# A hybrid attention block on one core: the key and value compression as whole fp32 products, two positions to a pass, with the positional encoding as extra columns

## The chip, the cores and the metric

The kernel runs on one core of a Trainium2 chip. The metric is the device time of one execution in microseconds (us); before the change it was run three times, and the median counts. The profile is of one further execution. Engine names: PE is TensorE's matmul queue and PEld its weight loads, DVE is VectorE, ACT is ScalarE, POOL is GpSimd, SP is SyncE, whose queue issues nearly all transfers. L12 is line 12 of the kernel file. "Granted clock" is the share of full speed that TensorE's clock was allowed.

## What is computed

One layer on a sequence of 1024 positions of width 1024: a mixer of two kinds of sparse attention, cross-attention to a memory of 256 rows, and an MLP of width 4096, each behind an RMS norm and added to the residual. The mixer projects the normed input with one wide matrix and splits the result. Only a small piece of it is touched by the change, the compressed keys and values of the second kind of attention:

```python
n_cmp = (L - CMP_BLOCK) // CMP_STRIDE + 1          # 63 blocks of 32 positions, stride 16
tok = jnp.arange(n_cmp)[:, None] * CMP_STRIDE + jnp.arange(CMP_BLOCK)[None, :]
k_blocks = k_br[:, :, 0][:, tok] + nsa_cmp_pe[0][:, None, :]
v_blocks = v_br[:, :, 0][:, tok] + nsa_cmp_pe[1][:, None, :]
k_c = jnp.einsum('bnlgd,lde->bnge', k_blocks, w_nsa_cmp[0])
v_c = jnp.einsum('bnlgd,lde->bnge', v_blocks, w_nsa_cmp[1])
k_c = _rope(_rms_norm(k_c, nsa_kn_g[0]), cmp_end)
```

So for keys and for values (kv = 0, 1), each of two heads g and each block n, 32 positions of 64 features, with an encoding of the position in the block added, are multiplied by 32 matrices of 64 x 64 and summed. The queries then attend to the 63 results, to selected blocks and to a window; the other kind of attention selects 256 positions by an index score. All inputs and outputs are fp32.

## The kernel before

**Number formats.** Most products are made in a reduced fp32 format of the PE (F32R in the code). An operand x is split into hi, its rounded copy, and lo = x - hi, and a product of two split operands is three matmuls: hi x hi, hi x lo, lo x hi. `split_w` (L240) splits weights: ACT makes hi, and POOL or DVE lo, by a rotating plan. Where both operands are left in plain F32 the product is one `matmul` in the code; these are called whole, and the projections of the second part and the output projections are done so (`load_whole`, L261). L218 is the helper through which every matmul passes, so in the profile nearly all of them carry this line and are told apart by their tiles.

**Stages.** The sequence is cut into two parts of four tiles of 128 positions (`PARTS`, L27). `project(pool, part, ...)` norms and transposes the part's input, and runs the wide projection in chunks of 256 columns (`gemm`, L300), handing each result bank to `consume`. Part 0 runs alone, in pool p1. Then attention starts on its tiles, and `together` (L110) interleaves it with a stream of other work, `fill`: the projection of part 1 (pool p2), the memory's projections, output projections, cross-attention and the MLP of the first four tiles. Every step of a generator announces a number (its rough cost), and `together` keeps attention and the other stream in proportion by these numbers and by `PACES` (1.35 for the first tiles). Attention's tile 3 is not begun before part 1 has been projected. The order in each engine's queue is settled when the kernel is built, by the tile framework's scheduler, which also inserts the waits.

**The compression.** Chunk 4 of the projection (columns 968 to 1223) holds the raw keys and values of the compressed branch. `consume` doubles each head's 64 features to 128 columns (L431), transposes (L434), and writes `KT[kv]`: features on the partitions, positions along the free dimension, hi on partitions 0 to 63 (ACT, L438, which writes all 128) and lo on 64 to 127 (DVE, L439). A matmul over 128 partitions so adds the products of hi and of lo in one pass, if the weights stand twice, above and below.

`compress` (L494) then goes over kv. It loads the 32 matrices as two tiles of 16, each transfer made twice for the upper and the lower half (L505), splits them in pieces of four positions (L511; ACT, POOL, DVE), and for each of the 16 offsets l in a stride of 16 multiplies by hi and by lo. The 128 weight columns are the matrices of position l and position l + 16, j = 0 and 1. The moving operand is `KT[kv][:, :, l::16]`, every sixteenth position, 64 columns in all for two heads and 32 strides (L515). Where part is 0, the same weights also multiply the encoding `pe`, two columns (L517), for the bias `cb` that both parts use. The two halves of the result, shifted by a block, are added to `cT` (L525 to L530), transposed, normed and rotated (keys) or split (values).

In part 0, `alternate` sends one projection tile of chunks 5 and 6 (8 tiles) and one step of `compress` (10 steps) by turns; in part 1 the two follow each other. In the profile the compression's bank is psC in part 0 and psD in part 1, `KT` is called c (tag c8, shared with other tiles), its weights come from tiles x (tag x4), and the encoding's bank is psM.

`pe_stack` (L1061) transposes the encoding at the start and splits it like `KT`.

Of the kernel before, what the change touches and what calls it, by code (L numbers as in the profile page):

```python
# [9 lines left out]
F32 = mybir.dt.float32  # L10
F32R = mybir.dt.float32r
# [11 lines left out]
P = 128  # L23
# [143 lines left out]
def build(nc, tc, I, C, out):  # L167
# [17 lines left out]
    def ring(pool, tag, shape, dt=F32):  # L185
        n = RINGS[pool.name if isinstance(pool.name, str) else "dn"][tag]
        return pool.tile(shape, dt, tag=tag, name=tag, bufs=n)
# [29 lines left out]
    def mm(o, a, b, start, stop):  # L217
        te.matmul(o, a, b, start=start, stop=stop)  # L218
# [149 lines left out]
    def project(pool, part, pe, st):  # L368
# [36 lines left out]
        def consume(ci, t, pt):  # L405
            T = t0 + t
            if ci in (0, 1):
                w = 256 if ci == 0 else 128
                gn = cqg if ci == 0 else ckvg
                ss = small(pool, "css", 1)  # L410
                raw = ring(pool, "relu", [P, 2, 256])
                s.activation(raw[:, 1, :w], pt[:, :w], AF.Square, accum_out=ss)
                s.activation(raw[:, 0, :w], pt[:, :w], AF.Copy)
                r = rsqrt_of(pool, ss, w, 1, "c")
                v.scalar_tensor_tensor(raw[:, 1, :w], raw[:, 0, :w], r[:, 0:1], gn, op0=ALU.mult, op1=ALU.mult)
                dst = [c[:, t, :, :] for c in cq] if ci == 0 else [c[:, t:t + 1, :] for c in ckv]
                to_T(pool, raw[:, 1, :], dst, w // P)
            if ci == 1:
                mu = small(pool, "mu", 1)
                v.tensor_reduce(mu, pt[:, 128:192], axis=AX.X, op=ALU.add)  # L420
                v.tensor_scalar(mu, mu, -1.0 / 64, None, op0=ALU.mult)
                v.tensor_scalar(kraw[t][:, IDX, :], pt[:, 128:192], mu[:, 0:1], None, op0=ALU.add)
                v.tensor_scalar(st["wi"][:, T, :], pt[:, 192:200], IDX_SCALE, None, op0=ALU.mult)
                s.activation(st["gi"][:, T, :], pt[:, 200:224], AF.Exp, scale=-1.0)
                v.tensor_scalar(st["gi"][:, T, :], st["gi"][:, T, :], 1.0, None, op0=ALU.add)
                v.reciprocal(st["gi"][:, T, :], st["gi"][:, T, :])
            if ci in (2, 3):
                stage_q(1, ci - 2, t, pt)
            if ci == 4:
                kd = ring(pool, "relu", [P, 4, 2, 64])  # L430
                s.activation(kd, pt.rearrange("p (a d) -> p a d", d=64)[:, :, None, :].to_broadcast([P, 4, 2, 64]), AF.Copy)  # L431
                p2 = pst("M", [P, 4, P])
                for a in range(4):
                    te.transpose(p2[:, a, :], kd[:, a, :, :].rearrange("p b d -> p (b d)"), ident)  # L434
                for kv in range(2):
                    dst = KT[kv][:, :, t * P:(t + 1) * P]
                    src = p2[:, kv * 2:kv * 2 + 2, :]
                    s.activation(dst, src, AF.Copy)  # L438
                    v.tensor_tensor(dst[64:128], src[64:128], dst[64:128], op=ALU.subtract)  # L439
            if ci in (5, 6):  # L440
                b = ci - 5
                V = st["V"][b]
                s.activation(kraw[t][:, 2 * b:2 * b + 2, :], pt[:, :128].rearrange("p (a d) -> p a d", d=64), AF.Copy)
                split_ps(pt[:, 128:256].rearrange("p (a d) -> p a d", d=64), V[:, T, :, 0, :], V[:, T, :, 1, :])
# [33 lines left out]
                    v.tensor_tensor(dst[64:128], p2[64:128], dst[64:128], op=ALU.subtract)  # L478
                yield 1.0

        KT += [ring(pool, "c8", [P, 2, nt * P], F32R) for _ in range(2)]
        yield from w_in([[(968, 256)]], 4)
        yield from w_in([[(0, 256)], [(256, 200), (1736, 24)]], 0)
        pair_ = (w_in([[(1224, 256)], [(1480, 256)]], 5), compress(pool, part, KT, pe, st, ctab))
# [9 lines left out]
    def compress(pool, part, KT, pe, st, ctab):  # L494
        t0, nt = PARTS[part]
        m0, nm = t0 * 8, nt * 8
        wc = W["w_nsa_cmp"].rearrange("k l d e -> k d l e")
        for kv in range(2):
            cp = pst(TAGS[pool.name][2], [P, 2, nm])
            pp = pst("M", [P, 2]) if part == 0 else None  # L500
            raws = []
            for j in range(2):
                raw = ring(pool, "x4", [P, 16, 64])
                for dup in range(2):
                    nc.sync.dma_start(raw[dup * 64:dup * 64 + 64], wc[kv][:, j * 16:j * 16 + 16, :])  # L505
                raws.append(raw)
            for rr in range(4):
                hi, lo = ring(pool, "whi", [P, 4, P], F32R), ring(pool, "wlo", [P, 4, P], F32R)
                for j in range(2):
                    js = slice(j * 64, j * 64 + 64)  # L510
                    split_w(raws[j][:, rr * 4:rr * 4 + 4, :], hi[:, :, js], lo[:, :, js])  # L511
                for r in range(4):
                    l = rr * 4 + r
                    for a, w in enumerate((hi, lo)):
                        mm(cp, w[:, r, :], KT[kv][:, :, l::16], l == 0 and a == 0, l == 15 and a == 1)  # L515
                    for a, w in enumerate((hi, lo) if part == 0 else ()):
                        mm(pp, w[:, r, :], pe[:, kv, l::16], l == 0 and a == 0, l == 15 and a == 1)  # L517
                yield 1.0
            cb = st["cb"][kv]
            if part == 0:  # L520
                b1 = small(pool, "cb1", 1, p=64)
                s.activation(b1, pp[64:128, 1:2], AF.Copy)
                v.tensor_tensor(cb, pp[0:64, 0:1], b1, op=ALU.add)
            cT = st["cT"][kv]
            s.activation(cT[:, :, m0:m0 + nm], cp[0:64], AF.Identity, bias=cb[:, 0:1])  # L525
            c1 = ring(pool, "relu", [P, 2, nm])[0:64]
            s.activation(c1, cp[64:128], AF.Copy)
            skip = 1 if part == 0 else 0
            dst = cT[:, :, m0 + skip - 1:m0 + nm - 1]
            v.tensor_tensor(dst, dst, c1[:, :, skip:], op=ALU.add)  # L530
            p2 = pst("M", [P, P])
            if kv == 0:
                te.transpose(p2[:, 0:64], cT.rearrange("p a n -> p (a n)"), ident[0:64, 0:64])
                ta = ring(pool, "relu", [P, 6, 64])
                ss = small(pool, "kcss", 1)
                s.activation(ta[:, 0, :], p2[:, 0:64], AF.Copy)
                s.activation(ta[:, 1, :], p2[:, 0:64], AF.Square, accum_out=ss)
                r = rsqrt_of(pool, ss, 64, 1, "kc")
                v.tensor_tensor(ta[:, 1, :], ta[:, 0, :], ctab[:, 0, :], op=ALU.mult)
                v.tensor_tensor(halves(ta[:, 2, :]), swap(ta[:, 0, :]), halves(ctab[:, 1, :]), op=ALU.mult)  # L540
                v.tensor_tensor(ta[:, 1, :], ta[:, 1, :], ta[:, 2, :], op=ALU.add)
                kcd = ta[:, 4:6, :]
                v.tensor_scalar(kcd, ta[:, 1:2, :].to_broadcast([P, 2, 64]), r[:, 0:1], None, op0=ALU.mult)
                p3 = pst("M", [P, 2, 64])
                te.transpose(p3.rearrange("p a n -> p (a n)"), kcd.rearrange("p a n -> p (a n)"), ident)
                Kc = st["Kc"][part] = at.tile([P, 2, 64], F32R, tag="Kc", name="Kc", bufs=len(PARTS))
                s.activation(Kc, p3, AF.Copy)
                v.tensor_tensor(Kc[64:128], p3[64:128], Kc[64:128], op=ALU.subtract)
            else:
                Vc = st["Vc"][part] = at.tile([64, 2, 2, 64], F32R, tag="Vc", name="Vc", bufs=len(PARTS))  # L550
                for gg in range(2):
                    te.transpose(p2[0:64, gg * 64:(gg + 1) * 64], cT[:, gg, :], ident[0:64, 0:64])
                split_ps(p2[0:64, :].rearrange("p (a d) -> p a d", a=2), Vc[:, :, 0, :], Vc[:, :, 1, :])
            yield 1.0
# [504 lines left out]
                    yield 2.6  # L1059

    def pe_stack():  # L1061
        pe = p1.tile([P, 2, 32], F32R, tag="pe", name="pe")
        pe2 = ring(p1, "relu", [P, 2, 2, 64])
        for j in range(2):
            nc.sync.dma_start(pe2[0:32, :, j, :], W["nsa_cmp_pe"].rearrange("k l d -> l k d"))
        pp = pst("M", [P, 2, 32])
        for kv in range(2):
            te.transpose(pp[:, kv, :], pe2[0:32, kv, :, :].rearrange("p a d -> p (a d)"), ident[0:32, 0:32])
        s.activation(pe, pp, AF.Copy)
        v.tensor_tensor(pe[64:128], pp[64:128], pe[64:128], op=ALU.subtract)  # L1070
        return pe

    st = {
# [78 lines left out]
```

## Time and profile before

| | |
|---|---|
| median of three runs | 1837.35 us (1835.46 to 1839.35) |
| profiled execution | 1835.75 us |
| its span, first to last instruction | 1833.9 us |
| mean granted clock | 0.970 |
| PE busy | 1726.9 us, 94% |
| ACT, DVE, POOL busy | 1074.6, 936.1, 895.0 us |
| HBM traffic | 101 GB/s over the span |

A row of a group reads: line, engine, operation, output tile <- input tiles, shapes, count, then busy time and mean duration of one, then the idle time of the engine ahead of them and what ended it. Durations of matmuls overlap, since they are pipelined; what one costs in a dense stream is the distance between the starts of two. A row of a stretch has the busy time of each engine in it, with the number of instructions in brackets, then the granted clock, the share of time in which the DMA engines were busy, and GB/s.

### The profile page before, as it was taken

How to read it: one execution, taken by the hardware profiler on the slowest of the kernel's cores; microseconds unless marked ns; L12 is line 12 of the kernel's file. 1: busy time of each engine (PE TensorE's matmuls, PEld its weight loads, DVE VectorE, ACT ScalarE, POOL GpSimd, SP SyncE). 2: the span in 40 equal slices, each digit the busy share in tenths (PEclk: the TensorE clock that was granted, in tenths of full speed). 3: DMA queues.
4: the chain of work that ended last, by engine and by line, in shares of the span. 5: the costliest groups of instructions: out<-in, count | busy, mean ns of one | idle time of the engine just before them, and what ended most of it. 6: DMA issues, size and time to landing. Idle time of an engine off the chain costs nothing. (4 is left out here: it accounts for less than half of the span.)

```text
span 1833.9 us, 28049 instructions
## 1 busy us (share of the span) xinstructions
PE 1726.9 (94%) x9262; PEld 1474.2 (80%) x9262; DVE 936.1 (51%) x2353; ACT 1074.6 (59%) x2687; POOL 895.0 (49%) x1034
## 2 busy tenths in 40 slices
PE   5996999889989998999999999999999799999999
PEld 5995988777878787778887788888988578787787
DVE  4553766575684678466664656646523422222222
ACT  4444658889588669955797457994412323333332
POOL 2364657446262244677676576662111144454443
PEclk9997998999999999999999999999989799999999
DMA  8224512256335320222112112125394222222232
GB/s 203 70 87 160 103 34 79 78 193 180 122 112 162 120 81 24 73 81 71 64 63 91 54 65 75 60 79 185 99 288 131 71 69 92 92 93 93 94 99 98
DMA packets 180081, 187.50 MB, mean 102 GB/s; under 512 B 34656, under 2 KB 149088, under 8 KB 179936
## 3 DMA queue, kind: packets, MB, share of 16 engines
q1 hardware_dynamic: 172000, 175.23, 30.8%
q0 software_dynamic: 7936, 10.49, 2.2%
q8 instruction: 73, 1.20, 0.3%
q14 instruction: 72, 0.59, 0.1%
HBM read 164.69 MB, written 20.97 MB: 101 GB/s over the span
## 5 line engine op out<-in xcount | busy, mean ns | idle before, releaser
L249 POOL TENSOR_TENSOR wlo<-wraw,whi 128x512 fp32r<-128x512 f32 (+1 forms) x230 | 308.5, 1347 | 278.7 <-ACT whi L244 247.6
L244 ACT ACTIVATE whi<-wraw 128x512 fp32r<-128x512 f32 (+2 forms) x289 | 181.1, 628 | 247.4 <-PE psS L218 147.1
L218 PE MATMUL psD<-whi,xh 128*128 128x256 f32 (+1 forms) x704 | 193.8, 359 | 3.6 <-ACT whi L244 2.9
L218 PE MATMUL psD<-wlo,xh 128*128 128x256 f32 (+1 forms) x704 | 194.8, 357 | 0.8 <-DMA wlo<-in_w_in_dram 0.8
L236 DVE TENSOR_TENSOR pl<-psPT,ph 128x512 fp32r<-128x512 f32 (+1 forms) x232 | 142.2, 621 | 78.2 <-ACT ph L235 75.4
L218 PE MATMUL psD<-whi,h 128*128 128x512 f32 x512 | 174.3, 404 | 1.8 <-POOL h L1037 1.0
L688 ACT ACTIVATE S<-S,mn 128x128 f32<-128x128 f32 (+7 forms) x192 | 142.7, 744 | 41.5 <-DVE mn L686 40.3
L218 PE MATMUL psS<-whi,h 128*128 128x512 f32 x512 | 162.1, 392 | 5.1 <-DVE b L899 5.1
L693 POOL TENSOR_SCALAR S<-S,sums,gi 128x640 f32<-128x640 f32 (+7 forms) x128 | 107.7, 850 | 106.7 <-DVE sums L691 99.0
L235 ACT ACTIVATE ph<-psPT 128x512 fp32r<-128x512 f32 (+1 forms) x232 | 122.8, 540 | 60.9 <-PE psPT L703 54.5
L249 DVE TENSOR_TENSOR wlo<-wraw,whi 128x512 fp32r<-128x512 f32 (+1 forms) x59 | 64.3, 1090 | 166.9 <-ACT whi L244 166.8
L218 PEld LDWEIGHTS psD<-whi,xh 128*128 128x128 f32 x704 | 134.0, 198 | 14.3 <-ACT whi L244 3.3
L218 PEld LDWEIGHTS psD<-wlo,xh 128*128 128x128 f32 x704 | 134.8, 197 | 12.5 <-DMA wlo<-in_w_in_dram 1.2
L703 PE MATMUL psPT<-c_ident,S 128*128 128x128 f32 x816 | 132.3, 279 | 8.3 <-DVE ql L236 4.2
L899 DVE TENSOR_TENSOR b<-psS,b 128x512 f32<-128x512 f32 (+1 forms) x80 | 50.0, 635 | 152.6 <-PE psS L218 152.6
L218 PEld LDWEIGHTS psS<-whi,h 128*128 128x128 f32 x512 | 96.1, 188 | 29.3 <-DVE b L899 9.3
L218 PE MATMUL psS<-K,qh 128*128 128x384 f32 (+3 forms) x288 | 113.5, 397 | 5.6 <-DVE mn L686 2.8
L218 PEld LDWEIGHTS psD<-whi,h 128*128 128x128 f32 x512 | 95.6, 190 | 23.7 <-DVE b L899 1.5
L703 PEld LDWEIGHTS psPT<-c_ident,S 128*128 128x128 f32 x816 | 98.1, 143 | 18.9 <-POOL S L693 5.6
L218 PE MATMUL psD<-wlo,h 128*128 128x512 f32 x256 | 102.5, 404 | 1.3 <-POOL wlo L249 1.3
L218 PE MATMUL psD<-xh,wlo 128*128 128x512 f32 x256 | 101.5, 398 | 0.0
L899 DVE TENSOR_TENSOR b<-psD,b 128x512 f32<-128x512 f32 (+1 forms) x112 | 63.2, 572 | 74.5 <-PE psD L218 73.0
(299 smaller groups left out, 4647.4 us busy)
## 6 DMA issues: line engine op xcount, KB each, us to landing
wraw<-in_w_ff_in_dram SPq DMA_DIRECT2D x128, 256.0 KB, 2.7
wraw<-in_w_ff_out_dram SPq DMA_DIRECT2D x128, 256.0 KB, 2.6
whi<-in_w_out_dram SPq DMA_DIRECT2D x32, 256.0 KB, 5.0
wlo<-in_w_out_dram SPq DMA_DIRECT2D x32, 256.0 KB, 4.6
wraw<-in_w_in_dram SPq DMA_DIRECT2D x24, 256.0 KB, 3.1
q<-st SPq DMA_DIRECT2D x12, 512.0 KB, 2.6
qin<-q SPq DMA_DIRECT2D x44, 128.0 KB, 2.3
x<-in_x_dram SPq DMA_DIRECT2D x8, 512.0 KB, 5.2
```

Of the source, the lines that this page charges most:

```text
L218: te.matmul(o, a, b, start=start, stop=stop)
L235: s.activation(hi, src, AF.Copy)
L236: v.tensor_tensor(lo, src, hi, op=ALU.subtract)
L244: s.activation(hi, raw, AF.Copy)
L249: (v if l == "v" else g).tensor_tensor(lo, raw, hi, op=ALU.subtract)
L688: s.activation(S, S, AF.Exp, bias=low, scale=-1.0, accum_out=sums[:, hh:hh + 1])
L693: g.tensor_scalar(Ss[hh], Ss[hh], sums[:, hh:hh + 1], 1.0 if gate is None else gate[:, hh:hh + 1], op0=ALU.mult, op1=ALU.mult)
L703: te.transpose(p2[:, j, hh, :], S[:, (c + j) * P:(c + j + 1) * P], ident)
L899: v.tensor_tensor(dst, pt, dst, op=ALU.add)
```

## The change

The compression is done in whole fp32 products, without split weights.

- `KT` becomes plain fp32. Its lower 64 partitions no longer hold lo but the same keys moved by one position: column c there is position c + 1. ACT writes the upper half (64 partitions), DVE copies the lower one from the bank.
- One pass then takes two positions, 2r on the upper partitions and 2r + 1 on the lower: the sum over 128 partitions adds both. 8 products per kv take the place of 16 offsets x 2 (hi, lo).
- The weights are loaded to match, even positions above, odd ones below, once each, and are used as loaded: one tile of type x4 per kv instead of two.
- In part 0 `KT` gets 16 more columns, into which POOL copies the encoding in the same stacked form. It is so multiplied as one more block per half, and the result has 2 x 33 columns instead of 2 x 32; the separate two-column products go.
- `compress` announces two steps of 1.0 per kv instead of five.

```diff
@@ consume, ci == 4
-                    dst = KT[kv][:, :, t * P:(t + 1) * P]
                     src = p2[:, kv * 2:kv * 2 + 2, :]
-                    s.activation(dst, src, AF.Copy)
-                    v.tensor_tensor(dst[64:128], src[64:128], dst[64:128], op=ALU.subtract)
+                    s.activation(KT[kv][0:64, :, t * P:(t + 1) * P], src[0:64], AF.Copy)
+                    v.tensor_copy(KT[kv][64:128, :, t * P:(t + 1) * P - 1], src[64:128, :, 1:])
@@ project
-        KT += [ring(pool, "c8", [P, 2, nt * P], F32R) for _ in range(2)]
+        KT += [ring(pool, "c8", [P, 2, nt * P + (0 if part else 16)]) for _ in range(2)]
+        for kv in range(0 if part else 2):
+            p3 = pe[:, kv, :].rearrange("p (a l) -> p a l", a=2)
+            g.tensor_copy(KT[kv][0:64, :, nt * P:], p3[0:64])
+            g.tensor_copy(KT[kv][64:128, :, nt * P:nt * P + 15], p3[64:128, :, 1:])
@@ compress
         for kv in range(2):
-            cp = pst(TAGS[pool.name][2], [P, 2, nm])
-            pp = pst("M", [P, 2]) if part == 0 else None
-            raws = []
+            n = nm + (1 if part == 0 else 0)
+            cp = pst(TAGS[pool.name][2], [P, 2, n])
+            raw = ring(pool, "x4", [P, 8, 2, 64])
             for j in range(2):
-                raw = ring(pool, "x4", [P, 16, 64])
-                for dup in range(2):
-                    nc.sync.dma_start(raw[dup * 64:dup * 64 + 64], wc[kv][:, j * 16:j * 16 + 16, :])
-                raws.append(raw)
-            for rr in range(4):
-                hi, lo = ring(pool, "whi", [P, 4, P], F32R), ring(pool, "wlo", [P, 4, P], F32R)
-                for j in range(2):
-                    js = slice(j * 64, j * 64 + 64)
-                    split_w(raws[j][:, rr * 4:rr * 4 + 4, :], hi[:, :, js], lo[:, :, js])
-                for r in range(4):
-                    l = rr * 4 + r
-                    for a, w in enumerate((hi, lo)):
-                        mm(cp, w[:, r, :], KT[kv][:, :, l::16], l == 0 and a == 0, l == 15 and a == 1)
-                    for a, w in enumerate((hi, lo) if part == 0 else ()):
-                        mm(pp, w[:, r, :], pe[:, kv, l::16], l == 0 and a == 0, l == 15 and a == 1)
-                yield 1.0
+                for odd in range(2):
+                    nc.sync.dma_start(raw[odd * 64:odd * 64 + 64, :, j, :], wc[kv][:, j * 16 + odd:j * 16 + 16:2, :])
+            for r in range(8):
+                mm(cp, raw[:, r].rearrange("p j e -> p (j e)"), KT[kv][:, :, 2 * r::16], r == 0, r == 7)
+            yield 1.0
             cb = st["cb"][kv]
             if part == 0:
                 b1 = small(pool, "cb1", 1, p=64)
-                s.activation(b1, pp[64:128, 1:2], AF.Copy)
-                v.tensor_tensor(cb, pp[0:64, 0:1], b1, op=ALU.add)
+                s.activation(b1, cp[64:128, 1, nm:n], AF.Copy)
+                v.tensor_tensor(cb, cp[0:64, 0, nm:n], b1, op=ALU.add)
             cT = st["cT"][kv]
-            s.activation(cT[:, :, m0:m0 + nm], cp[0:64], AF.Identity, bias=cb[:, 0:1])
+            s.activation(cT[:, :, m0:m0 + nm], cp[0:64, :, 0:nm], AF.Identity, bias=cb[:, 0:1])
             c1 = ring(pool, "relu", [P, 2, nm])[0:64]
-            s.activation(c1, cp[64:128], AF.Copy)
+            s.activation(c1, cp[64:128, :, 0:nm], AF.Copy)
@@ pe_stack
-        pe = p1.tile([P, 2, 32], F32R, tag="pe", name="pe")
+        pe = p1.tile([P, 2, 32], F32, tag="pe", name="pe")
...
         s.activation(pe, pp, AF.Copy)
-        v.tensor_tensor(pe[64:128], pp[64:128], pe[64:128], op=ALU.subtract)
```

## The prediction

> **What bounds the kernel now.** I read the page's busy times first, then the stages, then the lines of the compression, then single records.
>
> ```profile
> span 1833.9 us, 28049 instructions
> PE 1726.9 (94%) x9262; PEld 1474.2 (80%) x9262; DVE 936.1 (51%) x2353; ACT 1074.6 (59%) x2687; POOL 895.0 (49%) x1034
> ```
>
> TensorE is busy 94% of the span and no other engine reaches 60%. An average over stages proves little, so the stages (columns: stretch, its length, busy time of PE, PEld, DVE, ACT and POOL with their instructions, granted clock, DMA share, GB/s):
>
> ```profile
> 67.00:105.00 38.00, 37.82 (x314) 37.48 (x314) 14.45 (x37) 16.69 (x54) 11.05 (x13) 0.95 0.20 58
> 105.00:145.00 40.00, 38.12 (x312) 37.05 (x311) 22.37 (x40) 17.63 (x47) 23.35 (x22) 0.96 0.25 94
> 145.00:160.00 15.00, 2.24 (x9) 1.44 (x8) 3.27 (x8) 3.15 (x8) 5.19 (x6) 0.64 0.60 186
> 275.00:303.00 28.00, 25.51 (x151) 23.64 (x149) 18.23 (x58) 21.33 (x80) 18.03 (x30) 0.76 0.40 102
> 303.00:400.00 97.00, 87.41 (x451) 72.56 (x452) 65.12 (x184) 85.35 (x272) 52.64 (x73) 0.95 0.35 120
> ```
>
> The first part's compression lies in 67 to 105, beside the projection, with PE busy 37.82 of 38 us; the rest of that part, to 145, is PE's too (38.12 of 40). Then part 0 ends and the next stage starts from loads. The second part's compression lies in 275 to 303 amid attention: PE 25.51 of 28, ACT 21.33. After it ACT is nearly as full as PE (85.35 against 87.41 of 97).
>
> **What is removed on PE.** By lines and shapes (count | busy us, mean ns | idle before):
>
> ```profile
> L218 PE MATMUL psC<-c,wlo 128*128 128x64 f32 x32 | 8.8, 283 | 0.0
> L218 PE MATMUL psC<-c,whi 128*128 128x64 f32 x32 | 8.2, 270 | 0.0
> L218 PE MATMUL psM<-pe,wlo 128*128 128x2 f32 x32 | 8.0, 254 | 0.0
> L218 PE MATMUL psM<-pe,whi 128*128 128x2 f32 x32 | 8.0, 254 | 0.0
> L218 PE MATMUL psD<-c,whi 128*128 128x64 f32 x32 | 8.8, 306 | 0.0
> L218 PE MATMUL psD<-c,wlo 128*128 128x64 f32 x32 | 8.7, 306 | 0.2 <-POOL wlo L249 0.2
> ```
>
> That is 128 products in part 0 (64 of them two columns wide, the encoding) and 64 in part 1. The means overlap one another, so the price is the distance between starts (columns: start, us, engine):
>
> ```profile
> 93.06 0.28 PE L218 MATMUL psC<-c,wlo 128*128 128x64 f32 x1
> ...
> 94.39 0.34 PE L218 MATMUL psC<-c,wlo 128*128 128x64 f32 x1
> ```
>
> Twelve steps, of 2 and of 64 columns alike, take 1.33 us: 0.111 us each, whatever the width, so the weight load sets it. Part 0 loses 128 x 0.111 = 14.2 us of PE, part 1 64 x 0.111 = 7.1 us.
>
> **What is added on PE.** Two maps x 8 products = 16 whole fp32 products per part, of 66 columns in part 0 (64 and 2) and 64 in part 1. The kernel has whole products already: the output projection below makes 8 x 4 x 2 = 64 of them on this bank, and they stand as 128 records (this row and a like one), two to a product. The narrowest are 128 columns wide, in the small key-value projection:
>
> ```profile
> L218 PE MATMUL psS<-whi,b x64: 377/380/484, 1349.5 to 1378.8; 128*128 128x256 f32 x64
> 304.24 0.38 PE L218 MATMUL psD<-wlo,c 128*128 128x128 f32 x2
> 304.45 1.10 PE L218 MATMUL psD<-whi,xh 128*128 128x256 f32 x4
> 305.39 1.03 PE L218 MATMUL psD<-wlo,xh 128*128 128x256 f32 x4
> ```
>
> Two records of 128 columns take 304.45 - 304.24 = 0.21 us, one product; four of 256 take 0.94, so a product there is 0.47. Half the columns take half the time down to 0.105 a record, where the load's 0.111 is the floor. With 66 columns I take 2 x 0.11 = 0.22 us a product, 16 x 0.22 = 3.5 us a part.
>
> Upper end: the new products read every sixteenth column in more than one pass. The trace shows strided reading only for 64 columns inside 0.111 us, so at most 1.73 ns a column. A 256-column whole record takes twice the 0.111 of a single pass, so a record streams its columns twice: 132 x 1.73 = 0.229 us, 0.46 a product, 7.3 us a part. I keep 0.22, as the widths just quoted show the load as the floor. The Trainium skill ("SBUF — State Buffer", under the DMA port swizzle) says that SBUF has 16-byte cachelines and reading is free of penalty only up to a stride of 4 fp32, which speaks against these reads with stride 16; it gives no price, the old records have the same stride without showing one at 0.111, and by it the sum would move toward the upper end.
>
> Net on PE: 14.2 - 3.5 = 10.7 us in part 0, 7.1 - 3.5 = 3.6 us in part 1.
>
> **The clock.** Stretches cut at the changes of the granted clock (same columns as the stages):
>
> ```profile
> 91.00:94.40 3.40, 3.40 (x34) 3.40 (x32) 1.34 (x3) 1.45 (x5) 0.74 (x1) 1.00 0.02 5
> 94.40:97.80 3.40, 3.40 (x18) 3.40 (x18) 0.76 (x1) 1.03 (x3) 1.19 (x2) 0.51 0.01 2
> 101.40:104.80 3.40, 3.22 (x28) 3.08 (x28) 0.89 (x4) 1.89 (x8) 1.27 (x1) 0.99 0.73 213
> 104.80:108.20 3.40, 3.40 (x18) 3.01 (x17) 1.74 (x7) 1.70 (x8) 1.79 (x2) 0.51 0.35 106
> 285.50:289.00 3.50, 3.41 (x16) 2.97 (x16) 1.46 (x3) 3.50 (x15) 3.18 (x7) 0.52 0.03 5
> 292.50:302.60 10.10, 10.10 (x49) 10.04 (x48) 5.70 (x21) 6.78 (x26) 2.81 (x5) 0.50 0.58 173
> ```
>
> Half clock comes in pieces of 3.4 us, each losing about 1.7 us. Both pieces of part 0 follow 3.4 us in which PE was busy, but largely with products of 2 and 64 columns, which leave the array mostly empty for 0.111 us. Afterwards a block is 1.8 us of records streaming 132 columns, followed by a full projection tile. I expect both pieces to go: 3.4 us. Of the four pieces in part 1 (one in 285 to 289, three in 292 to 303), some follow waits for attention's own chains; I count one, 1.7 us. The Trainium skill ("TensorE: Matmul & The Clock Gate", Part 1) lets idle windows lower the clock; PE's 3.40 of 3.40 us ahead of the first piece disagrees, if idle means no record. By its rule the 5.1 us here would not come; that is a rival below.
>
> **Off PE.**
>
> ```profile
> L244 ACT ACTIVATE whi<-x x32: 399/411/421, 63.4 to 287.5; 128x256 fp32r<-128x256 f32 x32
> L249 POOL TENSOR_TENSOR wlo<-x,whi x24: 722/736/1203, 64.0 to 290.6; 128x256 fp32r<-128x256 f32 x24
> L249 DVE TENSOR_TENSOR wlo<-x,whi x8: 412/730/759, 65.2 to 95.8; 128x256 fp32r<-128x256 f32 x8
> L439 DVE TENSOR_TENSOR c<-psM,c x16: 427/427/429, 36.2 to 215.0; 64x256 fp32r<-64x256 f32 x16
> L505 SPq DMA_DIRECT2D x<-in_w_nsa_cmp_dram x16: 607/666/2597, 28.6 to 280.7; - x16
> ```
>
> The 32 splits of the compression's weights go: 32 x 0.41 = 13 us of ACT, 24 x 0.74 = 18 of POOL, 8 x 0.73 = 6 of DVE, all beside a busy PE. I book nothing for them; at best they shorten PE's waits in 275 to 303, 28 - 25.51 = 2.5 us. L439's subtraction becomes a copy of 254 columns that no longer waits for ACT, at most the 0.43 us of before, under PE's cover. Four small POOL copies put the encoding beside the keys; POOL is free early, and the nearest POOL row,
>
> ```profile
> L572 POOL TENSOR_TENSOR qtab<-c_sin,qgs 128x64 f32<-128x64 f32 x1 | 0.3, 314 | 0.0
> ```
>
> puts them between 0 and 4 x 0.31 = 1.3 us if the first weight splits queued behind them on POOL, and so PE, waited; I take nothing. The loads stay 16 but of half the size: every weight was fetched twice. SP's queue gets shorter; nothing is put ahead of another load. The rings of raw and split weights are used less, so later loads may start sooner. No wait is added.
>
> **Sum.** 10.7 + 3.4 + 3.6 + 1.7 = 19.4 us. The profiled execution took 1835.75 us (span 1833.9), so 1816.4; it lies 1.6 under the median 1837.35, on whose footing the forecast is 1818.0 us. A change under 0.2%, 3.7 us, can't be told from none.
>
> **Rivals.**
> *The clock stays as it is* (the granted clock is set by something else, or new pieces of half clock come elsewhere): only 14.3 us, 1823.0. For it: other pieces lie where no compression is (145 to 160 has 0.64). Chance 0.16.
> *Part 1's share is lost*: from 303 on ACT with 85.35 of 97 us sets the end of tile 3, and PE's saving becomes idle time. 10.7 + 3.4 = 14.1 us, 1823.3. Against it: PE is the fuller engine up to 303, and ACT's chain would start earlier with it. Chance 0.13.
> *Strided fp32 at the upper end*, 0.46 us a product (the same if a product stood as four records of 0.111, so not the two it is called): part 0 saves 14.2 - 7.3 = 6.9, part 1 loses 7.3 - 7.1 = 0.2, the clock gives 3.4: 10.1 us, 1827.3. Chance 0.09.
> *Slower: attention loses its cover.* The order is set at build from announced weights. Compression announces 4 units a part instead of 10, so attention's steps fall 6/1.35 = 4.4 units later relative to the projection, and part 1's work runs out earlier beside tiles 2 and 3, where ACT is nearly full. How thin PE gets there without cover shows in
>
> ```profile
> 380.00:390.00 10.00, 6.16 (x38) 5.08 (x37) 9.14 (x30) 9.12 (x27) 6.16 (x11) 0.90 0.92 313
> ```
>
> If all of 303 to 400 fell to that 0.62, PE would idle 37 us instead of 9.6: 27 us more, +8 net, 1845. It turns the sign where the stretch falls below 1 - (9.6 + 19.4)/97 = 0.70 busy. Against it: the memory's projections follow at once as new cover, and only 4.4 units move. Chance 0.14, of which 0.03 lies so near the turn that it is no change.
>
> **The numbers.** The forecast keeps 0.48. Faster: 0.48 + 0.16 + 0.13 + 0.07 (the strided case less 0.02 that ends within the bound) = 0.84; within 0.2%: 0.03 + 0.02 = 0.05; slower 0.11. The range: at best all six pieces of half clock (10.1 us) and the 2.5 us of waits go, 14.3 + 10.1 + 2.5 = 26.9, 1810, less the 2 us by which the runs before scatter and a little for earlier loads: 1807. Upward it takes in the strided case with its 1827 and part of the lost cover: 1831.
>
> **What would show it.** Right: 32 compression products in 64 records, about 0.11 us apart; no two-column records; the end of part 0's last projection, 145 now, near 131; granted clock 1.00 between 67 and 105; part 1's end earlier by 19 us. Wrong: fp32 records 0.2 us apart; half clock still around the blocks; the 145 mark moved but tile 4 starting when it did, or PE below 0.8 in the stretch that follows the second part's projection.

## The result and the profile after

The changed kernel takes 1809.38 us, median of four runs (1807.67 to 1813.34), against 1837.31 us: ratio 0.985, 95% interval 0.9832 to 0.9868. That is 27.9 us less, where 19.4 us were forecast; 1809.4 lies inside the range of 1807 to 1831. The page of the kernel after:

```profile
span 1806.0 us, 27690 instructions
PE 1700.2 (94%) x9134; PEld 1447.8 (80%) x9134; DVE 927.8 (51%) x2343; ACT 1061.9 (59%) x2655; POOL 887.4 (49%) x1015
```

PE is as full as before, with 128 records fewer. The new products, first as a group by tile, then as the third block of part 0 and what follows it (columns: start, us):

```profile
L218 PE MATMUL psC<-c,x x32: 273/292/294, 65.6 to 76.5; 128*128 128x66 f32 x32
74.76 1.99 PE L218 MATMUL psC<-c,x 128*128 128x66 f32 x16
76.50 0.37 PE L218 MATMUL psD<-whi,xh 128*128 128x256 f32 x1
```

32 records stand for 16 products, so two each, and 16 records take 76.50 - 74.76 = 1.74 us: 0.109 us a record, 0.218 a product.

Where the time came from shows in three landmarks that both kernels have: the first load of staged queries (part 0 is done), the last staging of queries (part 1 is projected), the last output of attention. First before, then after:

```profile
L564 SPq DMA_DIRECT2D qin<-q x44: 320/338/584, 147.8 to 1161.1; - x44
L403 SPq DMA_DIRECT2D q<-st x12: 319/320/439, 118.6 to 373.2; - x12
L717 SPq DMA_DIRECT2D o<-oc x64: 574/586/1124, 186.8 to 1330.6; - x64
```

```profile
L556 SPq DMA_DIRECT2D qin<-q x44: 319/339/1070, 133.3 to 1135.6; - x44
L403 SPq DMA_DIRECT2D q<-st x12: 319/320/343, 106.1 to 351.5; - x12
L709 SPq DMA_DIRECT2D o<-oc x64: 574/586/609, 172.0 to 1305.1; - x64
```

Part 0 ends 14.5 us earlier (147.8 to 133.3), part 1 is projected 21.7 us earlier, attention ends 25.5 us earlier, and the span 27.9. So half of the gain came after part 0.

A second way to split it: in stretches of 2 us I took PE's idle time, the clock's loss (length times one minus the granted share), and the rest, which stands for PE's work at full clock.

| us | PE idle | clock | work |
|---|---|---|---|
| before | 107.1 | 54.6 | 1672.2 |
| after | 105.8 | 42.7 | 1657.5 |
| difference | 1.3 | 11.9 | 14.7 |

Half clock that falls on idle time is counted twice here, and so is missing from the work. If the clock's loss is taken only where PE is busy, it goes from 45.2 to 32.4 us and the work from 1681.7 to 1667.8, which makes the differences 1.2, 12.8 and 13.9.

The clock around the two compressions (columns as in the prediction's stages; before, then after):

```profile
60.00:118.00 58.00, 57.82 (x476) 57.08 (x476) 27.48 (x72) 27.14 (x87) 24.32 (x26) 0.94 0.20 57
255.00:305.00 50.00, 47.51 (x276) 43.33 (x275) 30.46 (x102) 33.74 (x122) 29.21 (x47) 0.86 0.23 59
```

```profile
60.00:118.00 58.00, 56.94 (x495) 56.19 (x493) 30.61 (x77) 26.24 (x83) 27.54 (x25) 1.00 0.25 75
255.00:305.00 50.00, 49.42 (x298) 43.29 (x297) 36.39 (x117) 44.62 (x160) 31.38 (x46) 1.00 0.27 77
```

Every piece of half clock around them is gone: 3.4 us were lost in the first stretch and 6.8 in the second (four pieces of 3.41 us at half clock).

### The profile page after: what moved, and what is told of

Read it like the earlier page. It is cut to its first block, busy times and chain, and to the rows that moved or that the text cites. A ratio compares the mean times of both kernels' runs of the same rounds, so it can differ in the third digit from the quotient of the medians.

```text
span 1806.0 us, 27690 instructions
## 1 busy us (share of the span) xinstructions
PE 1700.2 (94%) x9134; PEld 1447.8 (80%) x9134; DVE 927.8 (51%) x2343; ACT 1061.9 (59%) x2655; POOL 887.4 (49%) x1015
## 5 line engine op out<-in xcount | busy, mean ns | idle before, releaser
L218 PE MATMUL psD<-wlo,xh 128*128 128x256 f32 (+1 forms) x704 | 190.3, 352 | 1.6 <-DMA wlo<-in_w_in_dram 1.0
L249 DVE TENSOR_TENSOR wlo<-wraw,whi 128x512 fp32r<-128x512 f32 (+1 forms) x58 | 56.3, 971 | 170.3 <-ACT whi L244 170.1
L218 PEld LDWEIGHTS psD<-whi,xh 128*128 128x128 f32 x704 | 130.0, 193 | 14.2 <-ACT whi L244 3.8
L695 PEld LDWEIGHTS psPT<-c_ident,S 128*128 128x128 f32 x816 | 97.6, 142 | 14.1 <-POOL S L685 4.5
```

The source lines that it names most:

```text
L249: (v if l == "v" else g).tensor_tensor(lo, raw, hi, op=ALU.subtract)
L695: te.transpose(p2[:, j, hh, :], S[:, (c + j) * P:(c + j + 1) * P], ident)
```

## The experiments

My theory after the result: PE's work gave the 14.7 us, and the narrow products had cost the clock in both parts. Its rivals: that the clock follows idle time only, that the splits on ACT and POOL had made PE wait, and that the later gain came from a shifted order.

### One part at a time

`NEW = (0,)` or `(1,)` picks the new code by part, and the old code stays for the other.

```diff
+            if part in NEW:
+                ...                      # whole fp32 products
+            else:
+                ...                      # hi and lo, as before
```

> The change in part 0 alone; part 1 as before. By the landmarks of the two traces part 0's end moved by 14.5 us (first query load 147.8 to 133.3), and if nothing later depends on it the time is 1837.3 - 14.5 = 1822.8. Rival (the gain after the second part's projection came from part 0's earlier end and shifted clock windows): 1837.3 - 14.5 - 6 = 1817 or below.

Measured: 1828.04 us, ratio 0.9953 (0.9937 to 0.997).

> The change in part 1 alone; part 0 as before. If all that the change gained beyond part 0 belongs to part 1: 27.9 - 14.5 = 13.4 us, 1823.9, with the half clock between 285 and 303 gone. Rival (only what was gained by the end of part 1's projection, 21.7 - 14.5 = 7.2 us, belongs to it): 1830.1. By the prediction's own terms 5.3 us: 1832.0.

Measured: 1847.4 us, ratio 1.0062 (1.0046 to 1.0078): slower than the kernel before. No theory had that. The landmarks, part 0 alone, then part 1 alone:

```profile
L590 SPq DMA_DIRECT2D qin<-q x44: 320/339/1288, 132.6 to 1155.9; - x44
L404 SPq DMA_DIRECT2D q<-st x12: 319/320/343, 105.7 to 364.5; - x12
```

```profile
L590 SPq DMA_DIRECT2D qin<-q x44: 319/338/592, 147.8 to 1161.8; - x44
L404 SPq DMA_DIRECT2D q<-st x12: 319/320/437, 119.7 to 358.9; - x12
```

Each part did what it should at its own place. Part 0 alone ends at 132.6, 15.2 us earlier. That its time is 5 us above the expected 1822.8 comes after. Its part 1 takes 364.5 - 132.6 = 231.9 us where the kernel before took 225.4, but its first cross-attention output, at 494.0, is again 16.8 us earlier than before (510.8). The stage from there to the end of attention then takes 831.2 us instead of 819.8; why is not shown. (Its profiled execution, 1832.54 us, was the slowest of its four.) Part 1 alone takes 358.9 - 147.8 = 211.1 us from there to its projected end, where the kernel before took 225.4. Its half clock is gone too, while with part 0 alone it is still there. The stretch of 255 to 305, part 0 alone, then part 1 alone:

```profile
255.00:305.00 50.00, 47.24 (x272) 42.94 (x271) 32.22 (x103) 40.92 (x150) 34.30 (x54) 0.86 0.27 72
```

```profile
255.00:305.00 50.00, 48.93 (x296) 43.40 (x295) 34.48 (x112) 38.05 (x139) 27.25 (x43) 1.00 0.20 57
```

What part 1 alone had gained, it lost after 490, in attention, where no line of it was edited.

### The old products with the encoding beside

```diff
-                        mm(pp, w[:, r, :], pe[:, kv, l::16], ...)
+        # KT of part 0 has 16 more columns, filled from pe; the bias is column nm of cp
```

> The kernel before with split weights and hi/lo operands, but with the encoding as extra columns in part 0, so that only the 64 two-column products go. PE work: 64 x 0.111 = 7.1 us. If few columns halve the clock, part 0's two pieces become fewer too: 1837.3 - 7.1 - 1.7 to 3.4 = 1826.8 to 1828.5; if only idle time does: 1830.2.

Measured: 1848.4 us, ratio 1.0066 (1.0046 to 1.0086). The first query load stands at 139.0, 8.8 us earlier, near the 7.1 us of the products left out. The rest went as with part 1 alone. In part 0 the clock is no better than before, so the fewer pieces that the first theory expected did not come:

```profile
60.00:118.00 58.00, 57.02 (x473) 56.29 (x472) 31.06 (x81) 28.72 (x94) 28.83 (x29) 0.94 0.27 75
```

So in this trace products of 64 to 66 columns in a single pass were narrow enough, among 128-column ones and with PE busy 3.32 of the 3.41 us ahead of the loss; two columns aren't needed for it.

### Width and stride, at the same count

Into the changed kernel's part 0 go 96 more products, whose results are not used:

```diff
+                for b in range(3):
+                    junk = pst("M", [P, 256])
+                    for i in range(16):
+                        mm(junk, xd[:, i % 8, 0:P], xd[:, i % 8, 0:256], i == 0, i == 15)
+                    yield 1.0
```

with `0:2` for two columns and `xd[:, :, i::16]` for 256 strided ones.

> The same 96 products, 256 columns wide, one after another in memory. Both theories: 96 x 0.111 = 10.7 us, 1820, granted clock 1.00 between 60 and 105. It differs from the two-column kernel in nothing but the width, so the distance of the two is the price of few columns: 0 by theory B, 1.7 to 5.1 us by theory A.

> The changed kernel with 96 more products in part 0's compression, six blocks of 16 between projection tiles, each only 2 columns wide; their results are not used. Theory A (few columns leave the array empty and so halve the clock, though PE has no gap): 96 x 0.111 = 10.7 us of PE plus one to three pieces of half clock of 1.7 us between 60 and 105, so 1809.4 + 12.4 to 15.8 = 1822 to 1825, granted clock under 0.97 in that stretch. Theory B (only idle time halves the clock): 10.7 us alone, 1820, granted clock 1.00 there.

> The kernel with 96 two-column products again, since its profiled execution ran at half clock from end to end. Theory A (few columns halve the clock): granted clock under 0.97 between 60 and 118, one to three pieces of 3.4 us. Theory B (only idle time does): 1.00 there, as with 256 columns. The first query load, 144.1 us in the 256-column kernel, then stands at 146 to 149 by A and 144 by B.

> The same 96 products, 256 columns wide, but every sixteenth element is read (stride 64 bytes). If a strided moving operand streams at full rate: 0.111 us a record and 1820, as with 256 columns in a row. If a stride beyond 4 fp32 is paid for: records over 0.15 us apart and at least 4 us more, 1824 or later; at twice the time a column 10.3 us more, 1830.

Measured: 256 columns 1833.45 us, ratio 0.9988 (0.9975 to 1.0002); two columns 1851.03 (median of three executions), and in the repetition 1847.17, ratio 1.0072 (1.0051 to 1.0094); strided 1842.78, ratio 1.0041 (1.0027 to 1.0054). The first profiled execution with two columns took 3408.16 us, with its two-column records 0.222 us apart instead of 0.112 although its granted clock reads 1.00; the other three took 1844.68 to 1851.88, hence the repetition. All are some 13 us or more above what was expected, and the loss lies where the section on the order finds it; the disputed prices are read in part 0 itself. The stretch of 85 to 120, two columns (the repetition), then 256:

```profile
85.00:120.00 35.00, 35.00 (x280) 34.69 (x278) 16.15 (x35) 13.60 (x42) 15.06 (x14) 0.90 0.18 51
```

```profile
85.00:120.00 35.00, 35.00 (x304) 34.58 (x303) 15.75 (x34) 13.06 (x42) 15.51 (x14) 1.00 0.24 75
```

PE is busy 35.00 of 35.00 us in both, and only the narrow products lose the clock: 10% of 35 us, two pieces in a row from 102.1. Theory A holds here, with one trace of each kernel. One block of 16 was not enough: the four that stand alone (at 71.5, 76.1, 80.6 and 93.1) left the clock at 1.00, and the loss follows the last two, which come one right behind the other (97.7 and 99.4). The Trainium skill ("TensorE: Matmul & The Clock Gate", Part 1) ties the drop to idle windows; with no gap between records in this stretch, the measurement decides against that reading, if idle means that no record runs.

The other traces fit one description of both cases. I cut the thirteen readable traces (all but the first with two columns) from 30 us on into the 3.41-us windows in which half clock starts and ends, and counted the columns that PE's records stream, by their shapes, in each window at full clock. None of the 6053 windows with 3200 columns or more was followed by half clock; 123 of the 148 with fewer than 2000 were. So the loss goes with few streamed columns, whether narrow products or gaps make them few.

The first query load of the 256-column kernel stands at 144.1, 10.8 us after that of the changed kernel (10.7 expected); with two columns at 145.0, between the 144 of B and the 146 to 149 of A, so this landmark decides nothing by itself. Its records came 0.106 us apart instead of 0.119, which is 96 x 0.013 = 1.2 us less, so the lost clock cost 145.0 - (144.1 - 1.2) = 2.1 us there. With the stride it stands at 152.4. One block of 16, 256 columns in a row, then with the stride:

```profile
72.46 2.06 PE L218 MATMUL psM<-xh 128*128 128x256 f32 x16
```

```profile
70.76 3.68 PE L218 MATMUL psM<-xh 128*128 128x256 f32 x16
```

Less the last record's length (0.28 and 0.40 us, the groups' means rounded) over 15 steps: 0.119 and 0.219 us a record. A stride of 64 bytes nearly doubles the time of streaming, to 0.86 ns a column. The Trainium skill ("SBUF — State Buffer", the cachelines under the DMA port swizzle) says that reading is free of penalty only up to a stride of 4 fp32; the trace agrees. The change doesn't feel it: 132 columns at 0.86 ns are 0.113 us, about what the weight load takes (0.111).

### The splits kept

The weights are split as before on ACT, POOL and DVE, and nothing reads the results.

```diff
+            for rr in range(4):
+                hi, lo = ring(pool, "whi", [P, 4, P], F32R), ring(pool, "wlo", [P, 4, P], F32R)
+                ...                      # split_w of both halves
```

> The changed kernel, with the splits of the compression's weights on ACT, POOL and DVE kept; nothing uses their results. If they were covered by PE before, as the prediction booked: 1809 to 1811, and the clock between 260 and 305 stays 1.00. Rival (ACT at 9.91 and POOL at 9.06 of 10 us in 280 to 290 before were what made PE wait and then lose the clock in part 1's compression): pieces of half clock come back between 262 and 300, 3 to 8 us more, 1812 to 1818.

Measured: 1826.4 us, ratio 0.9949 (0.9934 to 0.9965), 17 us above the changed kernel, further than either theory had it. The rival's mechanism isn't there:

```profile
255.00:305.00 50.00, 48.83 (x298) 43.26 (x297) 39.51 (x115) 43.64 (x158) 37.24 (x54) 1.00 0.31 93
```

The clock is whole with all that work on ACT and POOL, and the first query load (134.3) is 1.0 us late. The loss is later, again in attention. This kernel keeps the engines' load, but PE no longer waits for the splits; in the kernel before that wait was 0.2 us in part 1 (the last of the removed rows in the prediction). The changed kernel with three raw buffers, below, has the same order by the mark used there and takes 1824.28 us, so the splits themselves cost no more than some 2 us.

### The announced units

```diff
-            yield 1.0
+            yield 1.0 if part == 0 else 4.0
```

> The changed kernel, but part 1's compression announces 4.0 + 1.0 units per map as before, instead of 1.0 + 1.0. If the order of attention against the projection has no weight: 1809.4, within 2 us. Rival (the 6 units less let the projection run ahead and brought the gain that came later than 373, or cost some): 3 to 6 us away from 1809.4, upward if they helped.

Measured: 1811.99 us, ratio 0.9873 (0.9856 to 0.9889). That is 2.6 us above the changed kernel, between the 2 us of the one theory and the 3 to 6 of the other, and the intervals of the two ratios overlap. The announced units were not the cause of the later gain.

### The order behind them

In all kernels that came out too slow the loss lies between the first cross-attention outputs (476 to 510) and the end of attention. The queues' order there is settled at build; even one more fill of a constant, below, changes PE's order in 3907 lines. One mark sorts them: how many of attention's value products stand on PE ahead of the 1st, 65th, 129th and 193rd product of one kind in the first MLP half (lo weights of its second matrix).

```
arrangement 1   407 472 570 676   before, after, part 0 alone, units
arrangement 2   402 462 570 670   splits, encoding beside (403)
near it         402 462 570 671   part 1 alone, two columns
                402 462 570 676   256 columns, strided
```

Three kernels were then chosen by this mark before they ran. One changes PE's order but keeps arrangement 1; two get arrangement 2 (in one with 401 for 402) without a change of work, one from each kernel.

```diff
-    v.memset(mhalf, -0.5)
+    v.memset(mhalf, -0.5); v.memset(mhalf, -0.5)                 # before, arrangement 1
-PSUMS = {"p1": {"D": 4, "M": 3, "C": 1}, ...
+PSUMS = {"p1": {"D": 4, "M": 2, "C": 2}, ...                     # before, arrangement 2
-    "p1": {... "wraw": 4, ...
+    "p1": {... "wraw": 3, ...                                    # after, arrangement 2
```

> The kernel before with one more fill of a 128 x 1 constant (0.06 us of DVE) at the start. PE's order differs in 3907 lines but keeps the arrangement 407, 472, 570, 676. Theory (the arrangement decides, not each swap): within 5 us of 1836, PE idle 25 to 32 us in that stretch. Rival (any new order is a new draw of some 10 us either way): over 6 us away.

> The kernel before with part 0's result banks dealt otherwise (2 of the transposes' kind and 2 of the compression's instead of 3 and 1); no work is changed, the order of the queues comes out another. Its attention stands against the first MLP half as in the four slower experiments (the half's second column blocks start after 402, 462, 570 and 670 value products of attention, not 407, 472, 570 and 676). Theory (the order decides, and that arrangement costs PE about 13 us of waits between 480 and 1330): 1836 + 10 to 17 = 1846 to 1853, PE idle there 40 us or more instead of 27. Rival (order has no weight; the experiments were slower by their edits): within 4 us of 1836.

> The changed kernel with three instead of four buffers of raw weights in part 0; no work is changed, the order comes out in the slower arrangement (402, 462, 570, 670). Theory (order): 1809.4 + 10 to 17 = 1819 to 1826, PE idle over 40 us in attention behind the first output projections. Rival (the gain of 27.9 us belongs to the edit, and the order is nothing): within 4 us of 1809.4. Against the last-named kernel with the same arrangement the change should then be worth its PE work and clock, 22 to 29 us.

Measured: 1835.15 us, ratio 0.9993 (0.9979 to 1.0006); 1861.63 us, ratio 1.0125 (1.0088 to 1.0161); 1824.28 us, ratio 0.9942 (0.992 to 0.9964). The stage from the first cross-attention output to the end of attention, in arrangement 1 (before, before with the fill, after):

```profile
510.80:1330.60 819.80, 792.97 (x4300) 672.74 (x4298) 493.52 (x1226) 594.14 (x1386) 450.91 (x485) 0.99 0.27 87
```

```profile
506.20:1326.80 820.60, 791.15 (x4300) 670.45 (x4298) 492.82 (x1225) 593.51 (x1387) 450.77 (x485) 0.99 0.28 87
```

```profile
479.70:1305.10 825.40, 796.70 (x4330) 675.28 (x4328) 500.51 (x1238) 597.57 (x1399) 458.54 (x493) 0.99 0.28 87
```

and in arrangement 2 (before with other banks, after with three raw buffers, the splits kept):

```profile
509.30:1358.00 848.70, 806.99 (x4338) 687.71 (x4337) 489.86 (x1245) 599.70 (x1408) 455.69 (x495) 0.97 0.28 85
```

```profile
476.90:1318.60 841.70, 802.81 (x4337) 683.64 (x4337) 492.40 (x1244) 599.97 (x1408) 456.13 (x495) 0.98 0.28 86
```

```profile
476.20:1319.50 843.30, 800.81 (x4335) 680.90 (x4335) 492.14 (x1244) 600.29 (x1408) 455.86 (x495) 0.98 0.28 86
```

PE sits idle 27 to 30 us in the first three (length less busy time) and 39 to 43 in the others; in all thirteen traces it is 27 to 31 in arrangement 1 and 39 to 44 in the rest. No single wait holds the difference. Some of PE's waits in this stage, after, then after in arrangement 2 (columns: us in total, times, longest); all but the last grew:

```profile
PE psM L274 <- DMA relu<-xo: 4.5, 2, 3.9
PE psPV L218 <- DVE pl L236: 2.2, 5, 0.7
PE psM L274 <- DVE xl L236: 1.0, 2, 0.8
PE psPT L695 <- POOL S L685: 0.5, 2, 0.3
PE psM L274 <- DVE relu L297: 0.9, 2, 0.5
PE psS L218 <- DVE mn L678: 3.9, 6, 1.0
```

```profile
PE psM L274 <- DMA relu<-xo: 5.8, 3, 3.1
PE psPV L218 <- DVE pl L236: 3.6, 5, 1.4
PE psM L274 <- DVE xl L236: 3.6, 3, 3.0
PE psPT L695 <- POOL S L685: 2.5, 3, 1.4
PE psM L274 <- DVE relu L297: 2.4, 2, 2.1
PE psS L218 <- DVE mn L678: 2.5, 5, 0.9
```

They belong to cross-attention's short chains (transposes waiting for a norm or a reload) and to attention's softmax. That with the other interleaving PE has less other work just then is my reading and not shown. More clock is lost in this stage too, 20.5 us against 10.2.

Arrangement 2 cost the changed kernel 14.9 us, within the 10 to 17 expected. The kernel before lost 24.6 with other banks, more than expected, and the two kernels of arrangement 2 stand 37.4 us apart instead of 22 to 29. The banks' own place does not explain it: part 0 has one more piece of half clock, at 35 us, but its first query load stands at 148.8 (147.8 before) and its first cross-attention output at 509.3 (510.8 before), so all of the loss lies behind. Its four executions also scatter widely, from 1850.58 to 1867.67 us. So the mark tells the direction, not the size, and part 0 alone shows that it isn't all: it has arrangement 1 and 30.5 us of idle time, and still 11.4 us more in this stage than the kernel before. Why the scheduler falls into one arrangement or the other stays open.

## Why the prediction was right, and where its sizes were off

**PE's work, 14.3 us: right.** Measured 13.9 or 14.7, by the way of counting. A new product costs 0.218 us where 0.22 was taken from the 128-column rows and the load's floor. The upper end, 0.46 for strided reading, was far off: the bound of 1.73 ns a column came from records that waited for their weights, and the true price is 0.86.

**The clock in part 0, 3.4 us: right in size and in cause.** All five kernels with the old products in part 0 lose 1.7 to 5.2 us there; of the eight with the new ones only the two-column experiment does. Work and clock together, 14.1 us forecast, show at the first query load: it stands at 144.9 to 148.8 in the four kernels with the whole old part 0, and at 132.6 to 133.8 in the four whose part 0 is the changed one alone, 14.0 us apart in the mean.

**The clock in part 1, 1.7 us: the mis-sized term.** I counted one piece of four, because waits of attention's own chains stood ahead of some. Measured: all of it, 6.8 us. Five kernels with the old products in part 1 lose 5.0 to 8.5 us between 255 and 305; the eight with the new ones whose profile can be read lose none. The stretch from the first query load to the last staging of queries agrees: 223.3 to 231.9 us in the five, 211.1 to 218.2 in the eight, 12.6 us apart in the mean, where work and clock make 3.6 + 6.8 = 10.4.

The reading that waits stood ahead of the pieces was right; that they would stay was wrong. In the kernel before, three windows of part 1, the last two directly ahead of half clock, then PE's two long waits in those:

```profile
275.40:278.80 3.40, 3.40 (x29) 3.30 (x28) 3.33 (x10) 1.44 (x6) 2.07 (x5) 1.00 0.11 39
282.20:285.60 3.40, 2.25 (x13) 1.58 (x12) 2.04 (x9) 3.34 (x13) 2.78 (x5) 1.00 0.85 140
289.00:292.40 3.40, 2.30 (x21) 2.12 (x20) 3.37 (x11) 2.21 (x8) 3.40 (x6) 1.00 0.37 102
```

```profile
PE psM L533 <- DVE cT L530: 0.9, 1, 0.9
PE psPT L703 <- DVE ql L236: 1.1, 1, 1.1
```

In the first window 18 of the 27 products that start there have 64 columns, without a gap, and the clock stays whole. In the other two PE is idle for 1.1 us. One wait is the compression's own (L530 adds its halves), the other attention's. In the changed kernel no wait of PE there is over 0.3 us. As much idle time need not cost the clock: with other banks 284.9 to 288.3 has 1.1 us of it and full clock follows. So narrow products alone, shown to be enough in part 0, are not shown to be the cause in part 1: the waits, the narrow products around them, or both cost this clock, and no run separates them.

**Off PE, nothing booked: right.** Keeping all the splits moves part 0's end by 1.0 us and leaves the clock of both compressions alone.

Work and the clock of the two compressions make 14.7 + 3.4 + 6.8 = 24.9 of the 27.9 us; idle time gave 1.3, and the remaining 1.7 is clock elsewhere. This split is no finer than some 5 us: the kernel before with one more fill lost 43.0 us of clock, not 54.6, and was no faster. Three traces with all of the old work (before, with the fill, with other banks) lie at 1680 to 1686 us of work when the clock's loss is taken only where PE is busy, three with the new work (after, units, three raw buffers) at 1664 to 1669.

**The rivals.** That the clock stays, that part 1's share is lost, and that strided reading is dear for these products are refuted by the above. The slower rival, attention losing cover, was wrong in its cause (the announced units) and place (303 to 400), but an order that leaves attention less covered is real, and its price can exceed any term of the sum: the kernels in the other order lost some 13 to 25 us by it. That before and after lie in the same, better arrangement is luck, which nothing in the prediction had worked out. Each half of the change was not so steady: part 0 alone stays in it and gains 0.5%, part 1 alone leaves it and loses 0.6%. The prediction treated the order as a matter of 4.4 announced units, when even small edits can draw it anew. The changed kernel in the other arrangement, 1824.28, would still have lain in the range, but for a reason that none of its terms held.

The case for the change itself: within arrangement 1 it is worth 1.2 to 1.5% (0.985 against 1, 0.9873 against 0.9993). Within arrangement 2 the two kernels stand at 0.9942 and 1.0125, about 2% apart, with the wide scatter of the second.

## What to carry to other kernels

Price a matmul by its weight load when it is narrow: here a record costs 0.106 to 0.119 us from 2 to 256 columns streamed once and read in a row, so stacking two positions on the partitions and running fp32 whole beats hi and lo products that each stream 64 columns. Where a scheduler settles the order at build, an edit's effect at its own place (a landmark right behind it) and its effect on the order elsewhere are two measurements; run a version with the order changed and the work unchanged before believing a difference of 1%.

## What the runs showed of the hardware

The clock halved behind narrow products without a gap on PE: 35.00 us busy of 35.00, granted clock 0.90 with two-column products and 1.00 with 256 columns. One block of 16 two-column products (1.7 us) did not do it; two, one right behind the other, did. No 3.41-us window with 3200 or more streamed columns was followed by half clock, in thirteen traces. A moving operand read with a stride of 64 bytes streams at 0.219 us for 256 columns, in a row at 0.119.
